# Score matmuls with the keys' low parts on 64 partitions each, two units side by side

## The chip, the cores and the metric

The kernel runs on one core of a Trainium2 chip. The core has TensorE (PE in the profile, with its weight loads as PEld), VectorE (DVE), ScalarE (ACT), GpSimd (POOL) and the DMA queue of SyncE (SP). The metric is the device time of one execution in microseconds; the median of three runs of the kernel before is 1050.09 us (1049.32 to 1050.94).

## The reference, cut to what matters

The reference is one decoder layer over 512 positions: two token mixers (a gated linear recurrence and an attention with 16 heads in 4 groups), merged, and then an MLP. The change concerns the attention scores. Heads have 64 features; each head attends with two sets of keys ("selected" and "window", the branches), and since all eight blocks are selected and the window is as long as the sequence, both are causal attention over 512 positions:

```python
s_s = (jnp.einsum("bgrqd,bgqld->bgrql", qb, k_sel).astype(jnp.float32)
       + bias_gr[gi5, ri5, t5_bucket(dist_s)[:, :, None]])
p_s = masked_softmax(s_s, mask_s[:, :, None])
o_s = jnp.einsum("bgrql,bgqld->bgrqd", p_s.astype(v_sel.dtype), v_sel)
...
s_w = (jnp.einsum("bgrqd,bgsd->bgrqs", qb, kwb).astype(jnp.float32)
       + bias_gr[:, :, t5_bucket(dist_w)])
```

## The kernel before, in words

Matrix products are made from f32r operands, and every f32 operand is split into a high part and a low part, the rest; a product is the sum of high times high, high times low and low times high.

For the scores the two parts of the queries lie in the two halves of one tile. `q_step` makes it (`QS`, 128 partitions by 512 positions): the high part of a head's 64 features in one half of the partitions (the lower half for even heads, the upper for odd ones), the low part in the other. `k_step` makes `KK` with two planes, the keys' high part and their low part, each standing twice, in both halves; for the first group of heads ACT and DVE write the second copy, for the others a DMA on SP moves it. One matmul over 128 partitions of `QS` with the high plane thus gives (high + low) query times high key, and a second one, with the low plane, adds (high + low) query times low key. Both accumulate in one PSUM tile, `sc`.

For each head and branch `unit_a` is called three times. `UNITS` says which of the four blocks of 128 queries a unit holds: unit 0 block 3 (512 keys), unit 1 blocks 0 and 2 (128 and 384 keys), unit 2 block 1 (256 keys). So there are eight score matmuls for a head and branch, two each of 512, 128, 384 and 256 columns, at L943. After them `unit_a` does the softmax of the unit: bias and row minimum on DVE (L949), exponential on ACT (L951), normalisation and gate on POOL (L954). Three ticks later `unit_b` transposes the result on PE (L962) and `av_steps` multiplies by the values (L978, L981). `c_step` makes the scores with 31 compressed keys (L885).

PSUM has three buffers for `sc` (`SCB`), shared with `c_step`, three for the transposes (`pt`), one for `po` and one for the filler (`mf`). The filler are PE matmuls of other parts (gate projections, queries of the next group, the recurrence's output projection, L143 to L145) that `fill.pump` issues between the attention's steps. The order of instructions on each engine comes from a scheduler that runs a cost model; `issue_after` bars it from putting an instruction ahead of a given one, and `anchors` hold the last score matmul of each unit for that purpose.

The two bias tables are made earlier, in the recurrence stage, by two matmuls over 32 partitions in plain f32 (L468 and L473, two passes each). The recurrence's gates (`lru`, with `gwh` and `gwl`) use 112 partitions.

Of the kernel before, what the change touches and what calls it, by code (L numbers as in the profile page):

```python
# [11 lines left out]
F32 = mybir.dt.float32  # L12
F32R = mybir.dt.float32r
AF = mybir.ActivationFunctionType
# [4 lines left out]
T = 512  # L19
# [17 lines left out]
SCB = 3  # L37
LAG = 4
KB = 4
QB = 6  # L40
# [23 lines left out]
def f32(ap):  # L64
    return ap.bitcast(F32)
# [3 lines left out]
def layer(ctx, tc, x, norm_mix, w_in, conv_w, conv_b, gate_a_w, gate_a_b, gate_x_w, gate_x_b,  # L69
# [4 lines left out]
    V, S, G, PE, SP = nc.vector, nc.scalar, nc.gpsimd, nc.tensor, nc.sync  # L74

    def pool(name, side="left", space=None):
        kw = {} if space is None else {"space": space}
        return tc.tile_pool(name=name, bufs=1, side=side, reuse_waits="tile", **kw)
# [71 lines left out]
    class Cols:  # L150


        def __init__(self, w, starts):
            self.w, self.starts, self.got, self.raws, self.third = w, starts, {}, {}, None
            self.act = False
# [275 lines left out]
    qg = const.tile([128, 1], F32, name="qg")  # L431
# [35 lines left out]
    ps = psr.tile([128, T], F32, name="lru", bufs=4)  # L467
# [4 lines left out]
    ps = psr.tile([128, T], F32, name="lru", bufs=4)  # L472
# [200 lines left out]
    with pool("ph") as ph:  # L673
# [28 lines left out]
        for n, nm in enumerate("kv"):  # L702
            z = ph.tile([128, 4, T], F32, name="zd" + nm)
            G.memset(z[64:128, :, 496:512], 0.0)
            for m in range(2):
                ps = psr.tile([128, T], F32, name="mm", bufs=3)
# [3 lines left out]
                for gl in range(2):  # L710
                    g = 2 * m + gl
# [10 lines left out]
        for nm, w1, w2 in (("k", phi_k_w1, phi_k_w2), ("v", phi_v_w1, phi_v_w2)):  # L722
            ps = psr.tile([128, T], F32, name="lru", bufs=4)
# [23 lines left out]
            hs = ph.tile([128, 256], F32, name="hs")  # L747
# [6 lines left out]
            hl = ph.tile([128, 2, 128], F32R, name="hl")  # L754
# [4 lines left out]
            if nm == "k":  # L759
                ps = psr.tile([128, T], F32, name="lru", bufs=4)  # L760
# [14 lines left out]
            else:  # L775
                ps = psr.tile([128, T], F32, name="lru", bufs=4)
# [12 lines left out]
    psa = psa_es.enter_context(pool("psa", space=PSUM))  # L789
    yb_d = dram.tile([128, 8, T], F32, name="yb_d")  # L790
    at_es = ExitStack()
    at = at_es.enter_context(pool("at"))
# [38 lines left out]
    def add_q(g):  # L831
        fill.add(lambda: q_prep(g), lambda: q_gen(g))
# [4 lines left out]
    class Group:  # L837


        def __init__(self, g):  # L840
            self.g, self.K, self.Q, self.SC, self.PC = g, [None, None], [None] * 4, {}, None

        def k_step(self):

# [18 lines left out]
        def q_step(self, r2):  # L863

            pt = psa.tile([128, 4, 128], F32, name="pt", bufs=PTB)
            for i in range(4):
                PE.transpose(pt[:, i], QN[self.g][:, i, 128 * r2:128 * r2 + 128], ident)
            pf = pt.rearrange("p i t -> p (i t)")
            for j in range(2):
                q = at.tile([128, T], F32R, name="QS", bufs=QB)  # L870
                a, b = slice(64 * j, 64 * j + 64), slice(64 - 64 * j, 128 - 64 * j)
                S.activation(q[a], pf[a], AF.Copy, scale=qg[a])
                V.scalar_tensor_tensor(q[b], pf[a], qg[a], f32(q[a]), op0=OP.mult, op1=OP.subtract)
                self.Q[2 * r2 + j] = q

        def c_step(self, n):

            g = self.g
            ps = psa.tile([128, T], F32, name="sc", bufs=SCB)
            pv = ps.rearrange("p (j r x c) -> p j r x c", j=2, r=4, x=2)  # L880
            kc = KC[:, g].rearrange("p x c -> p (x c)")
            for j in range(2):
                ts = slice(128 * (2 * n + 1 - j), 128 * (2 * n + 2 - j))
                for r in range(4):
                    PE.matmul(pv[:, j, r].rearrange("p x c -> p (x c)"), self.Q[r][:, ts], kc, start=True, stop=True)  # L885
            sc = at.tile([128, 2, 4, 32], F32, name="scc", bufs=2)
            e = EC[:, 4 * g:4 * g + 4, 16 - 16 * n:48 - 16 * n]
            e = bass.AP(tensor=e.tensor, offset=e.offset, ap=[e.ap[0], [8, 2], e.ap[1], e.ap[2]])
            V.tensor_tensor(sc, pv[:, :, :, 0], e, op=OP.add)
            V.tensor_tensor(sc, sc, pv[:, :, :, 1], op=OP.add)  # L890
            mx = at.tile([128, 2, 4], F32, name="mxc", bufs=2)
            V.tensor_reduce(mx, sc, axis=AX, op=OP.min)
            s8, m8 = sc.rearrange("p j r c -> p (j r) c"), mx.rearrange("p j r -> p (j r)")
            mb = m8.unsqueeze(2).to_broadcast([128, 8, 32])
            G.tensor_tensor(s8, s8, mb, op=OP.subtract)
            S.activation(sc, sc, AF.Exp, scale=-1.0)
            V.tensor_reduce(mx, sc, axis=AX, op=OP.add)
            V.reciprocal(mx, mx)
            V.tensor_tensor(mx, mx, gates[:, 2 - 2 * n:4 - 2 * n].rearrange("p j (h c) -> p j h c", c=3)[:, :, 4 * g:4 * g + 4, 0],
                            op=OP.mult)  # L900
            G.tensor_tensor(s8, s8, mb, op=OP.mult)
            for j in range(2):
                self.SC[2 * n + 1 - j] = sc[:, j]
# [17 lines left out]
    def load_bias(h):  # L921
        bias_copies(h + BC)
        if h < 16:
            BTS[h] = at.tile([128, T], F32, name="BT", bufs=2)
            SP.dma_start(BTS[h], bass.AP(tensor=tab_p.tensor, offset=tab_p.offset + h * 128 * 640 + 127,
                                         ap=[[639, 128], [1, T]]))

    anchors = []
# [3 lines left out]
    UNITS = (((3, 0),), ((0, 0), (2, 128)), ((1, 0),))  # L932
    KT0 = (0, 768, 1152, 640)
    KTN = 1408

    def unit_a(grp, r, br, u):
        h = 4 * grp.g + r
        pp = at.tile([128, T], F32, name="pp", bufs=LAG + 2)
        ps = psa.tile([128, T], F32, name="sc", bufs=SCB)
        for i, c in UNITS[u]:  # L940
            ts, cs = slice(128 * i, 128 * i + 128), slice(c, c + 128 * (i + 1))
            for hl in range(2):
                ins = PE.matmul(ps[:, cs], grp.Q[r][:, ts], grp.K[br][:, hl, :128 * (i + 1)], start=hl == 0, stop=hl == 1)  # L943
        anchors.append(ins.ins)
        for i, c in UNITS[u]:
            cs = slice(c, c + 128 * (i + 1))
            mx = at.tile([128, 1], F32, name="mx", bufs=8)
            sm = at.tile([128, 1], F32, name="sm", bufs=8)
            V.tensor_tensor_reduce(out=pp[:, cs], in0=ps[:, cs], in1=BTS[h][:, 384 - 128 * i:],  # L949
                                   scale=1.0, scalar=3e38, op0=OP.add, op1=OP.min, accum_out=mx)  # L950
            S.activation(pp[:, cs], pp[:, cs], AF.Exp, bias=mx, scale=-1.0, accum_out=sm)  # L951
            V.reciprocal(sm, sm)  # L952
            gt = gates[:, 3 - i, 3 * h + 1 + br:3 * h + 2 + br]
            G.tensor_scalar(pp[:, cs], pp[:, cs], sm, gt, op0=OP.mult, op1=OP.mult)  # L954
        return pp
# [40 lines left out]
    grp = Group(0)  # L996
# [33 lines left out]
    for g in range(4):  # L1030
        nxt = Group(g + 1) if g < 3 else None
        for r in range(4):
            st = {}
            load_bias(4 * g + r + 2)
            for br in range(2):
                P = []
                for n in range(3):
                    pp = unit_a(grp, r, br, n)
                    fin = (av_steps(grp, r, br, P, st), grp) if n == 2 else None
                    pend.append([LAG - 1, n, pp, P, fin])  # L1040
                    if todo:
                        todo.pop(0)()
                    tick_back()
                    ev = EV.get(6 * r + 3 * br + n)
                    if nxt is not None and ev is not None:
                        if ev == "q0":
                            while (g + 1, 3) not in QN:
                                fill.pump(0.1)
                        {"q": nxt.q_step, "k": lambda _: nxt.k_step(), "c": nxt.c_step, "t": lambda _: nxt.ct_step()}[ev[0]](int(ev[1]))
                    if g == 0 and r == 0 and br == 0 and n < 3:  # L1050
                        fill.pump(RP)
                    w = work / 3 * WT[2 * r + br] / sum(WT) * GWT[g] / sum(GWT)
                    with tc.high_priority(offset=-FP):
                        if len(anchors) > AN:
                            with tc.issue_after(anchors[-1 - AN]):
                                fill.pump(w)
                        else:
                            fill.pump(w)
        if nxt is not None:
            for n in range(4 * g + 4, 4 * g + 8):  # L1060
                if n == 4 * g + 4 and g < 2:
                    add_q(g + 2)
                add_g(n)
        grp = nxt
# [156 lines left out]
    with pool("z", "right") as zp:  # L1221
# [10 lines left out]
        with pool("psm", space=PSUM) as psm:  # L1232
            for m in range(2, 32):
                wh, wl = MW.get(m)
                MW.prep(m + 1)
                ps = psm.tile([128, T], F32, name="mi", bufs=4)
                run(feat_gen(ps, wh, wl, TH, TL, lambda ps, m=m: relu2(m, ps)))
        with pool("psq", space=PSUM) as psq:
# [21 lines left out]
            for i in range(4):  # L1260
                for hf in range(2):
                    for f in (29, 30, 31):
                        mlp_mm(f, i, hf)
                    cs = slice(512 * hf, 512 * hf + 512)
# [46 lines left out]
```

## Time and profile before

| what | value |
|---|---|
| median of 3 runs | 1050.09 us (1049.32 to 1050.94) |
| the profiled execution | 1050.31 us |
| its span, first to last instruction | 1048.6 us |
| PE busy | 1030.1 us, 98% |
| DVE / ACT / POOL busy | 62% / 37% / 29% |
| granted clock of TensorE | 1.00 |

A row of the profile names an engine, a source line, an operation and, as out<-in, the tiles that it writes and reads; 128*128 is the size of the stationary operand (partitions by columns), and 128x512 f32 that of the result. Matmuls are pipelined: the duration of one contains latency, so the time that a matmul takes from PE is the distance from its start to the next one's. The chain that ended last is given from start to start. PE is the busiest engine throughout; the attention stage lies between 338 and 590 us.

### The profile page before, as it was taken

What the parts mean: (1) busy time and instruction counts of PE and PEld (TensorE: products, weight loads), DVE (VectorE), ACT (ScalarE), POOL (GpSimd) and SP (SyncE); (2) the same over time, 40 slices, a digit from 0 to 9 for tenths busy, and PEclk for the clock granted to TensorE, in tenths of its full rate; (3) what the DMA queues carried; (4) which work ended last, traced back from release to release, by engine and by line L of the source; (5) the groups of instructions that cost most, each with busy time, mean ns of one, the idle gap of its engine ahead of it and who ended that gap; (6) DMA issues with size and microseconds to landing.
All of it is one profiled execution on the core that took longest, in us unless ns stands there. A gap on an engine that the chain in (4) does not pass through costs nothing.

```text
span 1048.6 us, 14720 instructions
## 1 busy us (share of the span) xinstructions
PE 1030.1 (98%) x5405; PEld 879.2 (84%) x5405; DVE 646.4 (62%) x1211; ACT 391.2 (37%) x811; POOL 299.9 (29%) x346
## 2 busy tenths in 40 slices
PE   6999999999999999999999999999999999999998
PEld 5877877999888988989988888888888888888886
DVE  5688979837864877778687668554333343444443
ACT  4356666314433656747566621131111101111110
POOL 4210111420321655546545412211222121222110
PEclk9999999999999999999999999999999999999999
DMA  7646333654445533435333378402323232323222
GB/s 182 151 111 179 95 108 112 142 154 112 136 120 155 176 84 109 129 111 138 88 96 99 124 249 310 158 1 87 115 81 119 82 103 100 118 81 115 87 81 81
DMA packets 110039, 127.89 MB, mean 122 GB/s; under 512 B 23087, under 2 KB 87375, under 8 KB 109967
## 3 DMA queue, kind: packets, MB, share of 16 engines
q1 hardware_dynamic: 109967, 126.94, 40.6%
q8 instruction: 43, 0.70, 0.3%
q14 instruction: 29, 0.24, 0.1%
HBM read 109.45 MB, written 15.64 MB: 119 GB/s over the span
## 4 chain that ended last, share of the span: by engine, by line
PE 84%; DMA 5%; DVE 5%; issue 2%; ACT 2%; POOL 1%; SPq 0%; DVEq 0%; POOLq 0%; ACTq 0%
PE mf L143 6%; PE mf L144 6%; PE mf L145 6%; PE am L145 6%; PE am L143 6%; PE am L144 6%; PE mi L145 5%; PE mi L143 5%; PE mi L144 5%; PE sc L943 4%; PE po L981 4%; PE pt L962 3%; PE mm L144 3%; PE mm L143 3%; PE mm L145 3%; PE lru L143 3%
## 5 line engine op out<-in xcount | busy, mean ns | idle before, releaser
L139 DVE TENSOR_TENSOR wl<-wraw,wh 128x1024 fp32r<-128x1024 f32 (+2 forms) x110 | 132.5, 1206 | 65.4 <-POOL wh L138 49.6
L138 POOL TENSOR_SCALAR wh<-wraw 128x1024 fp32r<-128x1024 f32 (+3 forms) x83 | 85.7, 1033 | 252.9 <-PE mi L144 119.3
L954 POOL TENSOR_SCALAR pp<-pp,sm,gates 128x512 f32<-128x512 f32 (+3 forms) x128 | 92.9, 734 | 68.8 <-DVE sm L952 46.6
L144 PE MATMUL am<-mwl,zh 128*128 128x512 f32 x256 | 99.3, 389 | 0.0
L145 PE MATMUL am<-mwh,zl 128*128 128x512 f32 x256 | 99.3, 389 | 0.0
L143 PE MATMUL am<-mwh,zh 128*128 128x512 f32 x256 | 98.8, 389 | 0.0
L145 PE MATMUL mi<-XH,wl 128*128 128x512 f32 x240 | 93.5, 389 | 0.3 <-DVE wl L139 0.3
L143 PE MATMUL mi<-XH,wh 128*128 128x512 f32 x240 | 93.4, 389 | 0.1
L144 PE MATMUL mi<-XL,wh 128*128 128x512 f32 x240 | 93.4, 389 | 0.0
L1254 DVE TENSOR_TENSOR zl<-Z,zh 128x512 fp32r<-128x512 f32 x32 | 36.3, 1136 | 88.4 <-ACT zh L1253 88.4
L143 PE MATMUL mm<-XH,wh 128*128 128x512 f32 (+1 forms) x216 | 81.5, 379 | 1.1 <-DVE uc L336 1.1
L951 ACT ACTIVATE pp<-pp,mx 128x512 f32<-128x512 f32 (+3 forms) x128 | 71.5, 561 | 29.7 <-DVE mx L949 27.3
L144 PE MATMUL mm<-XL,wh 128*128 128x512 f32 (+1 forms) x216 | 81.5, 378 | 1.0 <-DVE XL L226 1.0
L145 PE MATMUL mm<-XH,wl 128*128 128x512 f32 (+1 forms) x216 | 81.1, 376 | 0.0
L1227 DVE SCALAR_TENSOR_TENSOR Z<-mi,zr 128x512 f32<-128x512 f32 x30 | 20.7, 691 | 97.2 <-ACT zr L1226 97.2
L138 POOL TENSOR_SCALAR mwh<-wraw 128x1024 fp32r<-128x1024 f32 x32 | 34.0, 1064 | 138.3 <-PE am L145 131.3
L1253 ACT ACTIVATE zh<-Z 128x512 fp32r<-128x512 f32 x32 | 20.2, 632 | 136.5 <-PE am L144 134.4
L1226 ACT ACTIVATE zr<-mi 128x512 f32<-128x512 f32 x30 | 18.0, 600 | 141.7 <-PE mi L145 136.9
L949 DVE CUSTOM_DVE_ANT_0 pp<-sc,BT 128x512 f32<-128x512 f32 (+3 forms) x128 | 59.0, 483 | 15.1 <-PE pt L962 7.3
L968 ACT ACTIVATE PH<-pt 128x512 fp32r<-128x512 f32 (+1 forms) x96 | 49.2, 524 | 33.0 <-PE pt L962 32.6
L969 DVE TENSOR_TENSOR PL<-pt,PH 128x512 fp32r<-128x512 f32 (+1 forms) x96 | 55.9, 592 | 6.1 <-ACT PH L968 6.0
L943 PE MATMUL sc<-KK,QS 128*128 128x512 f32 (+3 forms) x256 | 57.8, 334 | 0.0
(307 smaller groups left out, 2669.9 us busy)
## 6 DMA issues: line engine op xcount, KB each, us to landing
wraw<-in_w_in_dram SPq DMA_DIRECT2D x26, 1024.0 KB, 5.4
wraw<-in_w_mlp_in_dram SPq DMA_DIRECT2D x16, 1024.0 KB, 5.5
wraw<-in_w_mlp_out_dram SPq DMA_DIRECT2D x16, 1024.0 KB, 4.8
tab_p<-tab_t SPq DMA_DIRECT2D x16, 320.0 KB, 5.2
wraw<-in_proj_a_dram SPq DMA_DIRECT2D x8, 640.0 KB, 5.1
BT<-tab_p SPq DMA_DIRECT2D x16, 256.0 KB, 2.8
wraw<-in_proj_b_dram SPq DMA_DIRECT2D x4, 1024.0 KB, 5.2
wraw<-in_w_out_dram SPq DMA_DIRECT2D x4, 1024.0 KB, 5.2
```

The source lines that it names most:

```text
L138: G.tensor_scalar(h, v, 1.0, 0.0, op0=OP.mult, op1=OP.add)
L139: split_last[0] = V.tensor_tensor(l, v, f32(h), op=OP.subtract).ins
L143: PE.matmul(ps, lh, rh, start=start, stop=False)
L144: PE.matmul(ps, lh, rl, start=False, stop=False)
L145: return PE.matmul(ps, ll, rh, start=False, stop=stop)
L943: ins = PE.matmul(ps[:, cs], grp.Q[r][:, ts], grp.K[br][:, hl, :128 * (i + 1)], start=hl == 0, stop=hl == 1)
L949: V.tensor_tensor_reduce(out=pp[:, cs], in0=ps[:, cs], in1=BTS[h][:, 384 - 128 * i:], scale=1.0, scalar=3e38, op0=OP.add, op1=OP.min, accu ...
L951: S.activation(pp[:, cs], pp[:, cs], AF.Exp, bias=mx, scale=-1.0, accum_out=sm)
L954: G.tensor_scalar(pp[:, cs], pp[:, cs], sm, gt, op0=OP.mult, op1=OP.mult)
L968: S.activation(ph, pv, AF.Copy)
L969: V.tensor_tensor(pl, pv, f32(ph), op=OP.subtract)
L981: PE.matmul(po[:, 128 * kt:], VV[:, kt, br, g], P[n][:, KT0[kt]:KT0[kt] + 128 * (4 - kt)], start=False, stop=br == 1 and kt == 3 and n == 1)
```

## The change

A new function `scores` makes the matmuls, for units 0 and 1 together and for unit 2 alone. It first issues the matmuls with the keys' high plane, on 128 partitions as before; then those with the low plane. For units 0 and 1 these now take 64 partitions: unit 0 reads the half of `QS` that holds the high query part, and unit 1 a copy of that part in the opposite half, in a new tile `QO`. The product of the two low parts is no longer made for these two units. Unit 2 keeps 128 partitions. `q_step` makes `QO`: for the first group by an ACT copy, for the others by a DMA on SP. `unit_a` gets its PSUM tile from `scores`, so that two `sc` tiles are taken at once.

```diff
+            qo = at.tile([128, T], F32R, name="QO", bufs=QB // 2)
+            for j in range(2):
+                a, b = slice(64 * j, 64 * j + 64), slice(64 - 64 * j, 128 - 64 * j)
+                if self.g == 0:
+                    S.activation(qo[b], pf[a], AF.Copy, scale=qg[a])
+                else:
+                    SP.dma_start(f32(qo[b]), f32(self.Q[2 * r2 + j][a]))
+                self.QO[2 * r2 + j] = qo
...
-    def unit_a(grp, r, br, u):
+    def scores(grp, r, br, us):
+
+
+        out = [psa.tile([128, T], F32, name="sc", bufs=SCB) for _ in us]
+        K, Q = grp.K[br], grp.Q[r]
+        own = 64 * (r % 2)
+        es = ExitStack()
+        for hl in range(2):
+            if hl:
+                es.enter_context(tc.issue_after(ins.ins))
+            for n, (ps, u) in enumerate(zip(out, us)):
+                for k, (i, c) in enumerate(UNITS[u]):
+                    ts, cs = slice(128 * i, 128 * i + 128), slice(c, c + 128 * (i + 1))
+                    q, hs = Q, slice(0, 128)
+                    if hl and len(us) > 1:
+                        q, p = (Q, own) if n == 0 else (grp.QO[r], 64 - own)
+                        hs = slice(p, p + 64)
+
+                    ins = PE.matmul(ps[:, cs], q[hs, ts], K[hs, hl, :128 * (i + 1)], start=hl + k == 0,
+                                    stop=hl == 1 and k + 1 == len(UNITS[u]))
+        es.close()
+        anchors.append(ins.ins)
+        return out
+
+    def unit_a(grp, r, br, u, ps):
         h = 4 * grp.g + r
         pp = at.tile([128, T], F32, name="pp", bufs=LAG + 2)
-        ps = psa.tile([128, T], F32, name="sc", bufs=SCB)
-        for i, c in UNITS[u]:
-            ts, cs = slice(128 * i, 128 * i + 128), slice(c, c + 128 * (i + 1))
-            for hl in range(2):
-                ins = PE.matmul(ps[:, cs], grp.Q[r][:, ts], grp.K[br][:, hl, :128 * (i + 1)], start=hl == 0, stop=hl == 1)
-        anchors.append(ins.ins)
...
-                    pp = unit_a(grp, r, br, n)
+                    if n != 1:
+                        ready = scores(grp, r, br, (0, 1) if n == 0 else (2,))
+                    pp = unit_a(grp, r, br, n, ready.pop(0))
```

On PE, in the first group, the kernel before has the two matmuls of a block next to each other (unit 2 of one branch, then units 0 and 1 of the next):

```order
L943 MATMUL sc<-KK,QS 128x256 x2
L943 MATMUL sc<-KK,QS 128x512 x2
L978 MATMUL po<-PC_3346,VC 128x512
L962 MATMUL pt<-ident,pp 128x128 x4
L943 MATMUL sc<-KK,QS 128x128 x2
L943 MATMUL sc<-KK,QS 128x384 x2
```

Here "x2" is high plane, low plane. In the changed kernel, on PE in the first group:

```order
L963 MATMUL sc<-KK,QS 128x256 x2
L963 MATMUL sc<-KK,QS 128x512
L963 MATMUL sc<-KK,QS 128x128
L963 MATMUL sc<-KK,QS 128x384
L963 MATMUL sc<-KK,QS 128x512
L963 MATMUL sc<-KK,QO 128x128
L963 MATMUL sc<-KK,QO 128x384
L143 MATMUL mf<-wh,XH 128x256
```

The second 512 and the two that read `QO` are the ones on 64 partitions (the order shows the result's shape alone). They stand behind one another in 26 of the 32 pairs. In the other six the scheduler has put something between them; one of these, on PE in the second group:

```order
L963 MATMUL sc<-KK,QS 128x384
L144 MATMUL mf<-wl,XH 128x256
L963 MATMUL sc<-KK,QS 128x512
L145 MATMUL mf<-wh,XL 128x256
L963 MATMUL sc<-KK,QO 128x128
L963 MATMUL sc<-KK,QO 128x384
L989 MATMUL pt<-ident,pp 128x128 x4
```

A filler matmul on 128 partitions moved in between the two halves of the pair.

## Rows read from the trace of the kernel before

**Rows 1.** The page, part 1: busy time, share and instructions of each engine.

```profile
PE 1030.1 (98%) x5405; PEld 879.2 (84%) x5405; DVE 646.4 (62%) x1211; ACT 391.2 (37%) x811; POOL 299.9 (29%) x346
```

**Rows 2.** Busy time by stretch: PE, PEld, DVE, ACT, POOL, then clock and DMA.

```profile
338.00:590.00 252.00, 252.00 (x1603) 226.76 (x1602) 194.28 (x613) 161.03 (x429) 135.63 (x175) 1.00 0.39 115
...
sum 458.00, PE 453.48 PEld 376.76 DVE 210.06 ACT 67.72 POOL 91.88; mean PE 113.37 PEld 94.19 DVE 52.51 ACT 16.93 POOL 22.97
```

**Rows 3.** The chain that ended last, start and length in us of its score pieces.

```profile
585.88 0.23 PE sc L943
...
587.72 0.57 PE sc L943 x4
...
588.95 0.23 PE sc L943 x2
...
406.77 1.27 PE sc L943 x8
...
341.77 0.81 PE sc L885 x8
```

**Rows 4.** Timeline of PE and of its weight loads, 440 and 445 us.

```profile
440.38 0.23 PE L981 MATMUL po<-PH,VV 128*128 128x128 f32 x1
440.44 0.27 PE L981 MATMUL po<-PL,VV 128*128 128x128 f32 x1
...
444.92 0.28 PE L145 MATMUL mf<-wh,XL 128*128 128x256 f32 x1
...
444.94 0.46 PEld L962 LDWEIGHTS pt<-ident,pp 128*128 128x128 f32 x4
```

**Rows 5.** Timeline at a change from 112 to 128 partitions.

```profile
61.05 0.39 PE L145 MATMUL lru<-uh,gwl 112*112 112x512 f32 x1
61.05 0.19 PEld L143 LDWEIGHTS mm<-XH,wh 128*128 128x128 f32 x1
...
61.28 0.39 PE L143 MATMUL mm<-XH,wh 128*128 128x512 f32 x1
```

**Rows 6.** Timeline around the two bias tables (32 partitions, 16 columns).

```profile
67.54 0.39 PE L145 MATMUL lru<-uh,gwl 112*112 112x512 f32 x1
67.86 0.11 PEld L468 LDWEIGHTS lru<-wraw 32*16 32x16 f32 x2 [0.38 <-ACT ee L385]
67.86 1.03 PE L468 MATMUL lru<-wraw 32*16 32x512 f32 x2
...
68.73 0.99 PE L473 MATMUL lru<-wraw 32*16 32x496 f32 x2
...
69.65 0.19 PEld L144 LDWEIGHTS mm<-XL,wh 128*128 128x128 f32 x1 [0.82 <-issue]
69.65 0.50 PE L144 MATMUL mm<-XL,wh 128*128 128x512 f32 x1
```

**Rows 7.** Lines 872 and 860: durations ns min/median/max, and time to landing.

```profile
L872 ACT ACTIVATE QS<-pt,qg x16: 670/684/687, 331.8 to 525.5; 64x512 fp32r<-64x512 f32 x16
...
L860 SPq DMA_DIRECT2D KK<-KK x6: 482/482/498, 402.7 to 541.1; - x6
...
DMA to landing us min/median/max: 2.8/2.9/3.0
```

**Rows 8.** Tile sc, 338 to 590 us: who waited for it (us, times).

```profile
  DVE pp L949: 5.9, 6
```

More of the change, by code (lines that the diff above doesn't have):

```diff
@@ L840, in __init__ @@
         def __init__(self, g):
-            self.g, self.K, self.Q, self.SC, self.PC = g, [None, None], [None] * 4, {}, None
+            self.g, self.K, self.Q, self.QO, self.SC, self.PC = g, [None, None], [None] * 4, [None] * 4, {}, None
         def k_step(self):
```

## The prediction

> **What bounds the kernel now.** I read four views, coarse to fine. The page first: TensorE (PE) is busy 98% of the span, and no other engine is above 62% [rows 1]. Such a share says little by itself, since ends of matmuls are modelled. So, second, the busy time by stretch: in the attention stage (338 to 590 us), the only place that the change touches, PE is busy 252.00 of 252 us at a granted clock of 1.00, VectorE (DVE) 194, ScalarE (ACT) 161 [rows 2]. The stretches behind it are full too: 453.48 of 458 us from 590 us to the end [rows 2]. A microsecond that the attention stage loses on PE therefore reaches the end almost whole, and one that it saves is saved.
>
> Third, the chain that ended last, because its pieces run from start to start and so are real prices, where a matmul's own duration (0.39 us for 512 columns) contains a latency that the next one hides. A score matmul of 512 columns takes 0.23 us; the four of 128, 128, 384, 384 columns take 0.57 us; two of 256 take 0.23 us; the eight of one head and branch 1.27 us [rows 3]. There are 32 such eights (16 heads, two branches), about 40 us. Eight matmuls of only 64 columns take 0.81 us [rows 3], 0.10 each, though a 128-column one can follow another after 0.06 us [rows 4]: the weight load has a pace of 0.10 to 0.11 us and bounds small matmuls. A 128-column matmul with its load in the open is thus 0.11 us, and the 384 one is 0.57 / 2 - 0.11 = 0.175 us.
>
> Fourth, the timeline with weight loads, for the question on which all hangs: when may the next load start? In the ordinary case at the start of the matmul before it: at 61.05 us a matmul on 112 partitions starts, and the load for the next, on 128, in the same hundredth [rows 5]; the trace has some thirty such changes between 112 and 128 partitions, all alike. The trace has one other shape, 32 partitions by 16 columns, for the two bias tables, and there it is different. A matmul starts at 67.54, and the load of the 32-partition one only at 67.86: 0.32 us later, where the stream of 512 columns needs 0.23. On the way out the same: the four 32-partition passes start at 67.86 (two take 0.87 us, to 68.73, so the last two stream until about 68.73 + 0.87 x 496 / 512 = 69.57), and the load of the 128-partition matmul starts at 69.65; that matmul is 0.50 us long instead of 0.39, for it waits for that load [rows 6]. Inside the 32-partition group the second load lies beside the first pass, as usual. The row of the way in names ACT as the one that ended the wait, so that boundary alone could be a coincidence; on the way out the profile names nothing that was waited for.
>
> **The change part by part.** It replaces per head and branch the second matmuls of units 0 and 1 (512, and 128 + 384 columns) by ones on 64 partitions, from the two halves; unit 2 keeps its two.
>
> Removed from PE's stream: the second half of the first six, 0.23 + 0.285 = 0.515 us if the halves cost nothing; put in: the same columns on half the rows. If the halves run side by side, the unit 0 matmul (0.23 us) hides behind the unit 1 chain, or the reverse: load of 128 (0.11), its stream (0.06), load of 384 beginning with that stream (0.11), its stream (0.175): 0.11 + 0.11 + 0.175 = 0.395 us after unit 0's start. Saved: 0.515 - 0.395 = 0.12 us. If the first of these loads is also done ahead, 0.285 us, and 0.23 us is saved. No row shows loads for one half under a matmul on the other, so both ends stay; I take the middle, 0.17 us. The order shows that this can happen in 26 of the 32 pairs only: in six the scheduler puts other matmuls between the halves, as the third piece of the order shows, and there nothing is saved.
>
> Added: changes of shape. Going in costs 0.32 + 0.11 - 0.23 = 0.20 us by the rows of the tables (wait to 0.32, load of 0.11 in the open, against the usual 0.23). Going out costs 0.08 (69.57 to 69.65) + 0.11 (0.50 - 0.39) = 0.19 us [rows 6]. The other bound is nothing at all, as between 112 and 128 partitions [rows 5]. I take the first, for two reasons. 64 partitions use half of the array's rows, nearer in kind to 32 than to 112, which is nearly all of them; and the two places where the load waits agree, 0.09 and 0.08 us behind the stream's end. What speaks against: those matmuls are also plain f32 in two passes and only 16 columns wide. Plain f32 alone does not do it, because the transposes here are plain f32 too, and their load starts at 444.94 beside the matmul at 444.92 [rows 4]; two passes or 16 columns could.
>
> The Trainium skill has a rule for this: "TensorEngine Tiling (Array Packing)", section Key Properties, says that going to another tiling mode, not merely to another tile, drains TensorE. By that rule, the trace agrees at both table boundaries, 0.32 us to the load instead of none. The same skill, "TensorE: Matmul & The Clock Gate", section on packing small matmuls, measures packed row tiles as truly parallel (3.07 times for four); no run here shows it, and by it alone the change would be a gain.
>
> The count: 26 pairs stand together, with 2 changes of shape each, 52. The six broken ones have 4, 4, 4, 4, 6 and 6, together 28. Sum on PE: 26 x (0.39 - 0.17) = 5.7 us, and 28 x 0.195 = 5.5 us: 11.2 us longer.
>
> The rest is hidden or small. Four ACT copies for the first group's QO, 0.68 us each by the like copy of QS, and 12 moves on SP for the others, 2.9 us to land by the like move of KK [rows 7]. ACT has 91 of 252 us free [rows 2], and a copy stands six or more steps ahead of its use; behind an SP move that waits stand weight loads, which PE's filler matmuls need, but the move waits only for one ACT copy. If that cover is gone, PE waits for a landing, 2.9 us, in its whole queue, 12 times at worst; I cost it at nothing. Two score buffers of three are now taken at once, and unit 0's softmax starts some 0.5 us later; DVE waited for these scores 5.9 us in all [rows 8] and PE for nothing in this stage [rows 2], and DVE gets more slack when PE is slower. I keep 1 us either way for the new order.
>
> The profiled execution took 1050.31 us (span 1048.6 and 1.7 around it), 0.2 above the median of 1050.09 of the three runs. 1050.1 + 11.2 gives 1061.3 us.
>
> **Rivals.**
> No drain, halves side by side (the end on the other side): the waits at the tables belong to the two passes or to the 16 columns, and 64 partitions behave like 112. For it: those thirty free changes [rows 5]. Then 26 x 0.12 to 0.23 = 3.1 to 6.0 us go, 1044 to 1047 us; 1046 as the middle. The point from which it decides: a change of shape under 0.085 us (half of 0.17) makes the 26 pairs a gain.
> No drain, and no overlap: matmuls start in order, and the second half simply streams behind the first. Every matmul costs what it does now; 1050 us, within 1.
> Drain, and no overlap: 26 x 0.39 + 5.5 = 15.6 us, 1066 us. Against it: with separate halves and separate score banks nothing in sight orders them.
>
> **How the numbers follow.** Forecast (drain, side by side) 0.50, own range 1056 to 1066, since the saving may be 0.12 and the order worth 1 us (upper end) or a drain of two thirds (lower). Drain without overlap 0.09. Gain 0.29. Neither 0.12. So slower by over 0.2%, about 2 us, which is what a measurement of this kernel can tell from no change, 0.59; within that 0.12; faster 0.29. The range has to hold the gain too: 1045.0 to 1066.0 us.
>
> **What would show it.** Right: the loads of the first 64-partition matmul and of the matmul behind the pair start some 0.09 us after the stream before them has ended, in every pair; the chain has PE score pieces that are longer, about 1.5 us for an undisturbed eight; the attention stage ends about 11 us later, while the stretches behind it keep their lengths. The overlap shows as a unit 1 matmul that starts within 0.15 us of unit 0's. Wrong: loads of the halves begin beside the matmul before them (no drain), or unit 1's matmul starts 0.23 us behind unit 0's (no overlap), or PE waits in this stage for QO, for DVE or for a score bank, which none of the cases has.

## The result and the profile after

The changed kernel takes 1067.07 us (median of 6 runs, 1066.34 to 1068.47) where the kernel before takes 1050.06 in the same session: the ratio is 1.0159, 95% interval 1.0149 to 1.0169. It is slower by 17 us, 1.07 us above the top of the predicted range; 11.2 us slower was forecast. The profiled execution has a span of 1064.6 us, 16.0 more than before.

The loss falls in two places, not one. From the first score matmul to the first matmul of the output projection (`ao`) the kernel before needs 646.2 - 338.0 = 308.2 us, the changed one 656.5 - 338.7 = 317.8 us: 9.6 us more, where 11.2 were forecast. From the first `ao` matmul to the first of the MLP the trace gives another 5.7 us (706.70 - 646.21 = 60.49 before, 722.65 - 656.51 = 66.14 after), which no term of the prediction has. Busy time by stretch, changed kernel (PE, PEld, DVE, ACT, POOL, clock, DMA share, GB/s), answers to [rows 2]; the last three rows are cut out of the start of the output projection:

```profile
338.00:604.00 266.00, 265.60 (x1624) 226.77 (x1623) 200.63 (x625) 163.44 (x440) 131.10 (x176) 1.00 0.39 116
...
654.00:658.00 4.00, 4.00 (x18) 3.00 (x16) 3.14 (x5) 0.63 (x1) 0.00 (x0) 1.00 0.95 311
658.00:660.20 2.20, 0.03 (x1) 0.00 (x0) 0.77 (x2) 0.00 (x0) 0.00 (x0) 1.00 0.96 329
660.30:667.00 6.70, 5.53 (x13) 4.37 (x14) 3.70 (x6) 1.26 (x2) 0.00 (x0) 0.50 0.88 337
```

PE is as full as before in the attention stage, and that stage is longer: PE itself takes longer for the same 1867 matmuls between the two marks. Behind it PE stands still, through nearly the whole stretch from 658.00 to 660.20, and then the granted clock is 0.50, its lower level of 1.2 GHz, for 6.7 us.

**The pair, matmul by matmul.** The chain of the changed kernel, start and length in us, at the second piece of the order shown ahead of the prediction:

```profile
354.21 1.24 PE sc L963 x7
355.45 0.31 PE mf L143
355.77 0.12 PE mf L144
```

Seven pieces stand here for eight matmuls, because one of the 64-partition ones ends under another. An undisturbed eight took 1.27 us before [rows 3]; now it is 1.24 us, and the filler matmul behind it takes 0.31 where its neighbours take 0.12. Together 1.24 + 0.19 = 1.43 us, 0.16 us more for each pair that stands together. The timeline of PE and of its loads shows why:

```profile
354.90 0.32 PE L963 MATMUL sc<-KK,QO 64*128 64x128 f32 x1
```

```profile
354.90 0.18 PEld L963 LDWEIGHTS sc<-KK,QS 64*128 64x128 f32 x1 [0.19 <-issue]
354.90 0.29 PEld L963 LDWEIGHTS sc<-KK,QO 64*128 64x128 f32 x2
355.38 0.19 PEld L143 LDWEIGHTS mf<-wh,XH 128*128 128x128 f32 x1 [0.19 <-ACT PH L995]
355.49 0.19 PEld L144 LDWEIGHTS mf<-wl,XH 128*128 128x128 f32 x1
```

Two things are to be seen. The loads for both halves start in the same hundredth, 354.90, and unit 1's matmul starts there too: the halves do lie side by side. And the load queue is idle for 0.19 us ahead of the first 64-partition load and again ahead of the first 128-partition one, naming nothing that it waits for at the first (the second row names ACT): the loads that otherwise start with the matmul before them, as in [rows 5], wait here as at the bias tables [rows 6]. It is not this pair alone. The view of L963 lists the idle time ahead of all score loads for which the profile names no cause, in us and times:

```profile
  issue: 6.9, 37
```

That is 0.19 us each; the same view of the kernel before has no such line.

**The output projection.** The second place, in PE's and in DVE's timeline of the changed kernel:

```profile
657.64 0.39 PE L145 MATMUL ao<-owh,ML 128*128 128x512 f32 x1
661.47 0.79 PE L143 MATMUL ao<-owh,MH 128*128 128x512 f32 x1 [3.44 <-DVE gtb L1166]
662.06 0.63 PE L144 MATMUL ao<-owl,MH 128*128 128x512 f32 x1
...
667.12 0.39 PE L144 MATMUL ao<-owl,MH 128*128 128x512 f32 x1
```

```profile
659.40 0.69 DVE L1165 SCALAR_TENSOR_TENSOR gpa<-gta,gpa 128x512 f32<-128x512 f32 x1 [2.26 <-DMA gpa<-sp_pa]
660.12 0.69 DVE L1167 TENSOR_TENSOR gtb<-gtb,gpa 128x512 f32<-128x512 f32 x1
660.73 0.68 DVE L1166 SCALAR_TENSOR_TENSOR gtb<-gtb,sc 128x512 f32<-128x512 f32 x1
```

The third product of `ao` goes into the PSUM bank that held the last `sc` tile of the merge. DVE reads that tile at 660.73 (L1166), behind two instructions for the tile before it, the first of which waits 2.26 us for the stored projection `gpa`. So PE waits 3.44 us for a DVE instruction that stood in the queue behind another's wait. In the kernel before the same line stood ahead of the wait for `gpa`:

```profile
650.06 0.69 DVE L1137 SCALAR_TENSOR_TENSOR gtb<-gtb,sc 128x512 f32<-128x512 f32 x1 [1.55 <-DMA gtb<-sp_tb]
652.07 2.05 DVE L1136 SCALAR_TENSOR_TENSOR gpa<-gta,gpa 128x512 f32<-128x512 f32 x2 [1.32 <-DMA gpa<-sp_pa]
```

A second thing moved, and the order of DVE does not tell of it: which product of `ao` needs that bank. The kernel issues the eight products in a fixed order (`LATE`). In the changed kernel the third one waits for the bank; with the order of the kernel before it is the eighth, as the run b_late below shows by the product at which PE waits. The kernel before reaches its eighth product here, just behind the end of DVE's read (650.06 + 0.69 = 650.75):

```profile
650.98 0.39 PE L143 MATMUL ao<-owh,MH 128*128 128x512 f32 x1
```

Nothing in the change touches these lines. The order on DVE and the buffers of the tiles are the scheduler's choice; that both came out otherwise 50 us behind the attention stage is seen, why it chose so is not shown.

### The profile page after: what moved, and what is told of

Its sections match the earlier page's. It is cut to its first block, busy times and chain, and to the rows that moved or that the text cites. A ratio compares the mean times of both kernels' runs of the same rounds, so it can differ in the third digit from the quotient of the medians.

```text
span 1064.6 us, 14758 instructions
## 1 busy us (share of the span) xinstructions
PE 1042.1 (98%) x5405; PEld 877.5 (82%) x5405; DVE 648.0 (61%) x1211; ACT 392.4 (37%) x815; POOL 295.2 (28%) x346
## 4 chain that ended last, share of the span: by engine, by line
PE 86%; DVE 4%; DMA 4%; issue 2%; ACT 2%; SPq 1%; POOL 0%; DVEq 0%; ACTq 0%; POOLq 0%
PE mf L143 6%; PE mf L144 6%; PE mf L145 6%; PE am L143 5%; PE am L145 5%; PE am L144 5%; PE mi L145 5%; PE mi L144 5%; PE mi L143 5%; PE sc L963 4%; PE po L1008 4%; PE pt L989 3%; PE mm L144 3%; PE mm L143 3%; PE mm L145 3%; PE lru L143 3%
## 5 line engine op out<-in xcount | busy, mean ns | idle before, releaser
L981 POOL TENSOR_SCALAR pp<-pp,sm,gates 128x512 f32<-128x512 f32 (+3 forms) x128 | 86.0, 681 | 78.1 <-DVE sm L979 63.1
L138 POOL TENSOR_SCALAR mwh<-wraw 128x1024 fp32r<-128x1024 f32 x32 | 34.0, 1065 | 138.3 <-PE am L145 131.4
L145 PEld LDWEIGHTS am<-mwh,zl 128*128 128x128 f32 x256 | 48.1, 188 | 10.1
```

What stands on the lines that cost most here:

```text
L138: G.tensor_scalar(h, v, 1.0, 0.0, op0=OP.mult, op1=OP.add)
L145: return PE.matmul(ps, ll, rh, start=False, stop=stop)
```

## The experiments

Theory 1: a change between 128 and 64 partitions keeps the next weight load from lying beside the matmul before it and costs some 0.19 us, the overlap of the halves wins less than two such changes, and the rest of the loss is DVE's order at the merge. Its rivals stand in each expectation. "Pinned" below is this edit of the merge, which makes DVE read the last two PSUM results first (added lines alone, here and in the other cuts below):

```diff
+        tbi = V.scalar_tensor_tensor(tb, tb, 1.0, pb[m], op0=OP.add, op1=OP.mult)
+        if m == 6:
+            continue
+        with ExitStack() as es:
+            if m == 7:
+                es.enter_context(tc.issue_after(tbi.ins))
+            for mm in ((6, 7) if m == 7 else (m,)):
...
```

All ratios are to the kernel before on the same chip, whose median was between 1049.9 and 1051.5 us, so times of different rows are compared by their ratios; "stage" is the time from the first score matmul to the first `ao` matmul in the run's profile.

| run | us | ratio, 95% interval | stage us |
|---|---|---|---|
| before | 1050.06 | | 308.2 |
| changed | 1067.07 | 1.0159 [1.0149, 1.0169] | 317.8 |
| a_pin | 1061.5 | 1.0105 [1.009, 1.012] | 318.7 |
| a_full | 1052.61 | 1.0021 [1.001, 1.0032] | 309.2 |
| a_same | 1068.41 | 1.0172 [1.0139, 1.0206] | 323.7 |
| a_other | 1061.7 | 1.0107 [1.0092, 1.0122] | 317.3 |
| b_one64 | 1062.68 | 1.0107 [1.0083, 1.0131] | 320.0 |
| b_one96 | 1051.4 | 1.0002 [0.9986, 1.0018] | 308.2 |
| a_tight | 1060.8 | 1.0087 [1.0067, 1.0108] | 315.7 |
| b_pin | 1051.17 | 1.0001 [0.9987, 1.0015] | 308.5 |
| b_late | 1055.09 | 1.0045 [1.0027, 1.0063] | 307.9 |

**a_pin: the changed kernel, pinned.** The edit above.

> The changed kernel with one edit in the merge behind attention: of the last two of the eight column tiles DVE reads both PSUM results before it touches the data that SP still has to bring (in the changed kernel the last of these reads stands behind a product that waits for a load). Theory 1 (the attention stage lost about 10 us to changes of the tile's rows; the other 5.7 us are this one wait and the lowered clock behind it): 1061 us, 1060 to 1063, no wait of PE for the merge, and no clock below 1.00 there. Rival (the later attention stage collides with loads whatever DVE's order): 1066 to 1068.

1061.5 us, as theory 1 had it: 5.6 us of the 17 (5.7 by the ratios) go with DVE's order and the half clock behind it. It was wrong in one detail: a wait of PE remains,

```profile
659.43 0.50 PE L143 MATMUL ao<-owh,MH 128*128 128x512 f32 x1 [1.33 <-DVE gtb L1165]
```

1.33 us, since the third product still needs the bank and DVE reaches that read only at 658.70 even without the wait for a load. The clock stays at 1.00 after it. From the first `ao` matmul to the first of the MLP this run takes 61.5 us, 1.0 more than the kernel before.

**b_pin: the kernel before, pinned.** The same edit.

> The kernel before with the merge pinned as in a_pin: a control. Both theories: 1050 us within 1, since DVE already reads both results early there.

Ratio 1.0001: the edit does nothing where the order was good already, so the other pinned runs can be compared with the kernel before. PE's order is the same as before in every matmul.

**b_late: the kernel before with the changed kernel's order at the merge.**

```diff
+            if m == 7:
+                es.enter_context(tc.issue_after(sum6.ins))
+            V.scalar_tensor_tensor(tb, tb, 1.0, pb[m], op0=OP.add, op1=OP.mult)
+        sum6 = V.tensor_tensor(tb, tb, pm, op=OP.add)
```

> The kernel before, its scores untouched, with one edit in the merge: for the last column tile DVE reads the PSUM result only behind the sum of the tile before it, which waits for a load of the stored projection; that is the order that the scheduler made in the changed kernel. PE's order is that of the kernel before. Theory 1 (the 5.7 us behind the attention stage come from this order of DVE, not from the scores): 1051 + 4 to 7 us, about 1056, with one wait of PE of 2 to 4 us at the output projection and a lowered clock behind it. Rival (the wait arises because the attention stage is longer and shifts the loads): 1050 to 1052, no such wait.

1055.09 against 1049.91 us, 5.2 us slower (4.7 by the ratio, 2.8 to 6.6) with the scores and PE's order untouched. PE's wait, at the eighth product of `ao`, and the DVE timeline:

```profile
655.23 0.50 PE L143 MATMUL ao<-owh,MH 128*128 128x512 f32 x1 [3.87 <-DVE gtb L1140]
```

```profile
652.50 1.48 DVE L1136 SCALAR_TENSOR_TENSOR gpa<-gta,gpa 128x512 f32<-128x512 f32 x2 [3.75 <-DMA gpa<-sp_pa]
653.89 0.69 DVE L1141 TENSOR_TENSOR gtb<-gtb,gpa 128x512 f32<-128x512 f32 x1
654.50 0.68 DVE L1140 SCALAR_TENSOR_TENSOR gtb<-gtb,sc 128x512 f32<-128x512 f32 x1
```

The same three lines in the same order as after the change, with a wait of 3.87 us on PE, and the stretch behind it has a mean clock below 1:

```profile
655.00:662.00 7.00, 6.77 (x23) 5.43 (x24) 3.95 (x5) 0.88 (x2) 1.13 (x1) 0.76 0.69 243
```

So a loss of this size needs neither the 64 partitions nor the longer stage; the order on DVE is enough. The rival falls. But the path is not quite that of the changed kernel: here DVE itself waits longer (3.75 us against 2.26), and PE needs the bank five products later. In the changed kernel PE would have come to the third product at 657.87 and to the eighth 3.4 us later, at 661.28 (an estimate from its trace, fifteen matmuls of 0.227 us); the read ended at 661.41. By this estimate DVE's order would have made PE wait some 0.1 us there without the earlier need of the bank. No run moves the bank alone, so the two share the 5.7 us, and how is not shown.

**a_full, a_same, a_other: one order, three sizes.** These three (pinned) have the same instructions in the same order on PE. All issue the high plane of units 0 and 1 first and then the low plane, without `QO`; they differ in the partitions of the low plane's matmuls alone:

```diff
 # a_full
+                        hs = slice(0, 128)
 # a_same
+                        hs = slice(own, own + 64)
 # a_other
+                        p = own if n == 0 else 64 - own
+                        hs = slice(p, p + 64)
```

> As a_pin, but the second matmuls of units 0 and 1 keep 128 partitions, without QO: only the new order is left (high plane of both units first, then the low plane). Theory 1: the order costs nothing in PE's stream, 1050 us, 1049 to 1052. Rival (the regrouping itself, with two score banks taken at once, costs part of the 10 us): 1054 or more.

> The same instructions in the same order as a_full, but the second matmuls of units 0 and 1 take 64 partitions, all from the same half, so none can lie beside another. The order has 78 changes between 128 and 64 partitions. Theory 1 (each change of the rows costs 0.19 to 0.20 us): a_full + 15 us, about 1065. Rival (changes of shape are free, the loss comes with the overlap or the order): as a_full, 1050.

> The same instructions in the same order as a_full and a_same, but unit 0 takes one half and unit 1 the other (there the low part of the queries: unit 1's products with the keys' low part use the wrong query part, for the time alone). Theory 1: 27 trios stand together and win 0.2 us each by lying side by side: a_same - 5.5 us, about 1060. Rival (the halves do not overlap): as a_same, 1065.

a_full is 0.2% slower (1052.61 us, just above its expected range; its stage is 1.0 us longer, 0.7 against b_pin): the new order alone costs 1 to 2 us. a_same against it prices the changes: (323.7 - 309.2) / 78 = 0.186 us each. a_other against a_same prices the overlap: (323.7 - 317.3) / 27 = 0.24 us for each trio (the one low-plane matmul of unit 0 and the two of unit 1) that stands together. The three runs have the same order on PE, DVE, ACT and POOL, so the prices compare like with like. a_same's total, 1068.41 us, lies 3 us above the expected 1065: its profile has another wait for `gtb` at the output projection,

```profile
PE ao L143 <- DVE gtb L1156: 2.6, 1, 2.6
```

so the stage, not the total, is the fair measure.

**b_one64 and b_one96: how many partitions.** The kernel before, pinned, in its own order; only unit 2's second matmul changes:

```diff
+ # b_one64
+                hs = slice(64 * (r % 2), 64 * (r % 2) + 64) if u == 2 and hl else slice(0, 128)
+ # b_one96
+                hs = slice(0, 96) if u == 2 and hl else slice(0, 128)
+                ins = PE.matmul(ps[:, cs], grp.Q[r][hs, ts], grp.K[br][hs, hl, :128 * (i + 1)], start=hl == 0, stop=hl == 1)
```

> The kernel before (merge pinned as in a_pin), with one edit: unit 2's second matmul takes 64 partitions (the half with the high part of the queries), alone, so there are 64 changes of rows and nothing to lie side by side. The order is that of the kernel before. Theory 1 (a change costs 0.19 to 0.20 us): 1050 + 12.5 = 1062.5 us, 1061 to 1064. Rival (at the bias tables it was the two passes or the 16 columns): 1050.

> As b_one64, in the same order, but that matmul takes 96 partitions (leaves out a quarter of its products). Theory 1 in its narrow form (what counts is whether the rows fit half of the array; 112 did not pay): 1050 us, 1049 to 1051. Rival (any size that is a multiple of 32 and not 128 pays): 1062.5.

64 partitions: 1062.68 us, the expected 1062.5; 96 partitions: no difference. An undisturbed eight in the chain of b_one64 and then of b_one96:

```profile
373.67 1.67 PE sc L944 x8
```

```profile
370.89 1.28 PE sc L944 x8
```

0.39 us for a matmul that became smaller by half, and two changes in it: 0.195 each; the stage gives (320.0 - 308.5) / 64 = 0.18. The load queue's idle time in b_one64 is put down to nothing ("issue"), with no such row in b_one96; 15 loads are listed, and the other changes have 0.12 to 0.13 us each, too short for this list:

```profile
  issue: 3.1, 15
```

These matmuls are f32r, one pass and 128 columns of weights, so neither the two passes nor the 16 columns of the bias tables are needed for the effect.

**a_tight: the changed kernel, pinned, with the pairs held together.**

```diff
+                es.enter_context(tc.high_priority(offset=1000))
```

> a_pin with a high priority for the second matmuls of units 0 and 1, so that 31 of the 32 trios stand together instead of 26, with 66 changes of rows instead of 80. Theory 1: 31 trios at 0.17 us and one broken one at 0.8: 6 us over the kernel before, 1056 us, 1055 to 1058. Rival (the loss is not in the changes of shape): no better than a_pin, 1061.

1060.8 us, hardly better than a_pin: the expectation of theory 1 missed by 5 us, 1.5 of which are the chip (the kernel before took 1051.54 us there). Against that the loss is 9.3 us instead of 6. Its stage is 3.0 us shorter than a_pin's (315.7 against 318.7), but 7.2 us longer than the control's 308.5 instead of the 6 expected; its profile has two waits near the end of the attention part, 0.55 us for DVE and 0.56 us for POOL. From the first `ao` matmul to the first of the MLP it takes 61.0 us, 1.1 more than the control. The profiled execution also waits far ahead of the scores, in the recurrence, and reaches the first score matmul at 341.4 us, where the control does at 337.8:

```profile
49.22 0.65 PE L143 MATMUL mm<-XH,wh 128*128 128x512 f32 x1 [2.85 <-DVE uc L336]
```

with a granted clock of 0.50 for 3.4 us after it (mean 0.998 over the run). Of the four runs two have a mean clock of 0.998 (1061.82 and 1061.44 us) and two of 1.000 (1060.17 and 1059.67), 1.7 us apart; that the wait makes this difference is likely and not shown. Of the 9.3 us, 7.2 are the stage and 1.1 the output projection; about 1 us stays open. That fewer changes shorten the stage is shown; that the kernel as a whole gains what the prices say is not.

## Why the prediction was wrong

Right, by its own steps:
- The mechanism in the stage. Loads wait at each change between 128 and 64 partitions, in and out, and b_one64 against b_one96 excludes the other readings of [rows 6]. The term of 0.195 us measured 0.18 to 0.19. Two rows of a matmul of another shape, in another stage, were a better guide than the thirty free changes at 112 partitions.
- The overlap. Taken as 0.17 between 0.12 and 0.23, it measured 0.24: the upper end, because both first loads of a pair start together at 354.90. So a pair that stands together costs 0.13 us by the prices and 0.16 in the chain, not 0.22. The measured time is nearest to that of the rival with a drain and no overlap, 1066 us, but a_other against a_same shows the overlap: the total alone would have pointed to the wrong mechanism.
- The count of 26 and 6 pairs and 80 changes. With the measured prices: 80 x 0.186 - 26 x 0.24 = 8.6 us, and 1.0 for the regrouping that a_full shows, 9.6 us; the stage grew by 9.6. That it fits to the tenth is luck: a_pin, with the same order on PE, has a stage 0.9 us longer.
- What was hidden stayed so in the attention stage: the ACT copies, the moves of `QO` and the score banks. Its only wait of PE is one of 0.3 us for DVE (`QS`), and a_full has it too.

Wrong: the step "I keep 1 us either way for the new order", and with it the statement that "the stretches behind it keep their lengths". The order cost 1.0 us in the stage (a_full) and 5.7 us behind it. That term was sized at 1 us from the waits of the attention stage, but the order of every engine and the buffers of its tiles are open until the end of the program, and the edge that broke was at the merge: a PSUM read that PE needs, queued on DVE behind an instruction that waits for a DMA, for a bank that PE now needs at the third product and not at the eighth. The wait of 3.44 us was followed by a stretch at half clock. That DVE's order matters is shown by putting it into the kernel before (b_late, 5.2 us) and by taking it out of the changed one (a_pin, 5.6 us); the part of the bank is read from the traces and not tested. The order of DVE could have been read before the run; the prediction read the order on PE alone.

So of 17.0 us, some 9.6 are the stage and some 5.7 the merge. Of the rest, 0.6 us lies ahead of the first score matmul (338.04 before, 338.65 after; the other runs but a_tight have 337.6 to 338.7), 0.1 behind the start of the MLP, and 1.0 is the difference between the profiled executions (16.0 us apart) and the medians.

Two things about the numbers. The forecast was 1.6 us too high in the stage, and this hid some of the 5.7 us that it had not: that the result lies only 1.07 us above the range is luck. And the range's upper end does not follow from its terms: with 0.12 us saved a pair and 1 us for the order, 26 x 0.27 + 5.5 + 1 = 13.5 us, the prediction's own sum ends at 1063.6, not 1066.

## What to carry to other kernels

Splitting matmuls into half-height ones pays only if the change of height is rare: here two changes (0.37 us) stood against an overlap of 0.24 us for a trio. By these prices, an estimate that no run tests, at least two such trios would have to stand between two changes to win. Where a scheduler sets the order, compare the order of all engines to the end of the program, above all instructions that free PSUM for PE and stand behind one that waits for a transfer, and look which matmul needs the freed bank first.

## What was not expected of the hardware

The two halves' loads and first matmuls start within the same hundredth of a microsecond, although each load by itself has a pace of 0.10 to 0.11 us in this kernel [rows 3]. And 96 partitions cost nothing where 64 cost 0.39 us for a single matmul; the rows ahead of the prediction had only 32 and 112 to go by.
